# Hybrid attention and convolution layer: values loaded in shared chunks of three rows, and the order of the side work in the input projection

## The chip, the cores and the metric

One core of a Trainium2 chip runs the whole layer. The metric is the device time in microseconds (us) of one execution. The profile used here is of one execution of the same program.

## The reference

The layer takes 2048 latent tokens (a grid of 32 rows of 64) of width 1024 and 256 context tokens, all in float32:

```python
hx = modulate(rms_norm(x, norm1_g), sh1, sc1)
hc = modulate(rms_norm(ctx, norm1_g), csh1, csc1)
qx, kx, vx, ux = split_proj(hx @ w_in)              # 512, 512, 512 and 1024 columns
kc, vc = split_heads(hc @ w_in[:, 512:1536])
attn_x = neighbourhood_attention(rope(qx), qx, rope(kx), vx, kc, vc, rpb)
conv_x = conformer_conv(ux, dw_kernel, dw_bias, conv_ln_g, conv_ln_b)
x = x + g1 * (concat([attn_x, conv_x]) @ w_out)
x = x + g2 * (relu(modulate(rms_norm(x, norm2_g), sh2, sc2) @ w_mlp1) ** 2 @ w_mlp2)
out = rms_norm(x, final_g)
```

In the attention each token of row r attends to a window of 8 rows by 16 columns around it, with a learned bias by relative place (rpb), and to all 256 context keys, in one softmax. The convolution is a depthwise one of width 31 over the tokens, after a gated unit and before a LayerNorm. The vectors sh, sc and g come from products with w_ada.

## The kernel before

Float32 operands are split into a high and a low half, and each product is three matmuls (`mm3`, lines 90 to 92). The program has three stages: the input projection, the attention, and the output projection with the MLP. All data loads and stores stand in one queue, that of SyncE (SP), and are issued in its order.

**Input projection.** The tokens form two blocks of 1024 (b = 0, 1), each of two halves of 512 (`hf`). For each block the loop goes over ten groups of weight columns: four u groups (gated unit), two q, two k, two v; `half(gi, hf)` computes one group for one half. A half of a u group is 96 matmuls of 256 columns, a half of a q or k group 48 of 512 columns. Results go to DRAM: `h_d` (input of the convolution), `q_d`, `k_d`, `v_d`. Between the main matmuls stands side work:

- The convolution (`Conv`) works on pieces of 98 tokens by a Fourier transform: `load` reads a piece of h_d into `cw` and splits it on ACT and DVE (lines 416 to 418), `fwd` and `inv` are matmuls, `turn` transposes and stores. One piece is advanced in each half of q, k and v. `conv_tables` loads the transform's tables (`dftr`, `dwr`) and makes their product at line 396.
- `bias_tables` and `bias_rows` make tables of the attention's bias in DRAM: for each of 8 heads two loads (`tb`), an addition on GpSimd (POOL) and four stores, and then twelve larger copies from DRAM to DRAM into `bias_d` (line 299).
- `ada_chunk` computes a modulation vector on DVE from 16 loads of w_ada (`wr`). `pump` takes steps of it from a list, at a rate per half given by RATE.
- `load_x_half` loads four tiles of x for the next half or block and normalises them.

The scratch tiles of most of this (`gtile`, tag G) share one ring of four buffers. A scheduler decides the place of each instruction on its engine.

**Attention.** `groups_` lists 64 pairs p = (pr, hf, g): head pair pr (4 of them), column half hf, and row group g of four rows (8 of them). Its window is 11 rows of 40 columns (8 rows in the first and the last group). For a pair PE does scores (lines 986 and 988), transposes of the probabilities (lines 1024 and 1044) and the products with the values (lines 1062 and 1064), spread over three steps of a software pipeline (CYCLE). The values of a pair are loaded by one DMA, in chunks of three rows (120 partitions):

```python
v = ap.tile([P, 4, 2, P], F32R, tag="v", bufs=4, name=f"v{pr}{hf}{g}")
n = (nr + 2) // 3
src = v_d[hf * VW + r0 * 40:hf * VW + r0 * 40 + n * 120, pr * 256:(pr + 1) * 256]
```

r0 is 0 for the first group, 4g-4 for the others, so that the windows of neighbouring groups overlap by seven rows, and each loads its own copy. The queries of a pair (`q`, three buffers) are loaded two pairs ahead, the values one pair ahead (`loads`). The same queue also carries the next head pair's keys (`kr`), the bias tiles, and the stores of the results (`at_d`).

Of the kernel before, what the change touches and what calls it, by code (L numbers as in the profile page):

```python
# [18 lines left out]
P = 128  # L19
# [22 lines left out]
def hybrid_layer(ctx: ExitStack, tc: tile.TileContext, a: dict, out: bass.AP):  # L42
# [225 lines left out]
    def bias_tables():  # L268
# [4 lines left out]
        cm = gtile([64, 40], F32, "cm")  # L273
        SY.dma_start(cm, a["colmask"])
        neg = gtile([64, 120], F32, "neg")
        GE.memset(neg, NEG)
        SY.dma_start(z_d[0:32 * ZL].rearrange("(c l) -> c l", c=32)[:, 0:120 * 96],
                     rp_d.rearrange("a b -> (a b)").partition_broadcast(32))
        tiv = ti_d.rearrange("h f c n -> f c h n")
        for q in range(8):  # L280
            tb = gtile([64, 15, 40], F32, f"tb{q}")
            for hf in range(2):
                off = 32 + 15 - 8 * hf + q * 15 * 96
                src = z_d[off:off + 32 * (ZL - 1)].rearrange("(c l) -> c l", c=32)[:, 0:15 * 96]
                SY.dma_start(tb[hf * 32:hf * 32 + 32, :, :],
                             src.rearrange("c (h x) -> c h x", x=96)[:, :, 0:40])
            GE.tensor_tensor(tb, tb, cm.unsqueeze(1).broadcast_to([64, 15, 40]), ALU.add)
            for hf in range(2):
                src = tb[hf * 32:hf * 32 + 32, :, :].rearrange("p r c -> p (r c)")
                SY.dma_start(tf_d[q, hf], src)  # L290
                SY.dma_start(ti_d[q, hf][:, 120:440], src[:, 120:440])
# [93 lines left out]
    def conv_tables():  # L385
        ab = pa.tile([P, 2, 512], F32, name="cab")
# [6 lines left out]
        SY.dma_start(raw_[0:CW, 1, 0:2 * P], a["dft_k"])  # L393
        pt = psA("pab")
# [7 lines left out]
        z = gtile([P, 512], F32, "hz")  # L402
        GE.memset(z, 0.0)
        SY.dma_start(h_d[0:PAD], z[0:PAD])
        SY.dma_start(h_d[PAD + S:HR], z[0:HR - PAD - S])
        held = []
        cvc.update(ab=ab, br=br, hl=hl, held=held, ps=psA("pcv", held))

    class Conv:
# [47 lines left out]
    def conv_a(last):  # L457
        i = cv_pos[0]
        for d, fn in ((2, Conv.turn), (1, Conv.inv)):
            if cvc and 0 <= i - d < last and not hasattr(cvs[i - d], f"did{d}"):  # L460
                setattr(cvs[i - d], f"did{d}", True)
                fn(cvs[i - d])

    def conv_b(last):
# [7 lines left out]
        if i < last + 2:  # L472
            cv_pos[0] += 1
# [46 lines left out]
    def load_x_half(b, hf):  # L520
        tiles = []
        for i in range(4):
# [10 lines left out]
            tiles.append(xt)  # L533
        scale, shift = norm_mod(tiles, Ar, Br, f"n{b}{hf}")
# [142 lines left out]
    def before(gi):  # L677
# [3 lines left out]
        if gi == 0:  # L681
            xt1 = load_x_half(0, 1)
# [13 lines left out]
    def half(gi, hf):  # L696
# [3 lines left out]
        if kind == "u":  # L700
# [13 lines left out]
            if ct == 3 and hf == 1:  # L714
                cv_pos[0] = (0, CB0)[b]
                conv_b(CBS[b])
        elif kind in "qk":
            pt = psA(f"p{kind}{b}{idx}{hf}")
            for j in range(2):
                (conv_a, conv_b)[j](CBS[b])  # L720
# [3 lines left out]
            rope_store(b, kind, idx, hf, pt)  # L724
        else:
            for t2 in range(2):
# [4 lines left out]
                (conv_a, conv_b)[t2](CBS[b])  # L731
                if idx == 1 and hf == 1 and b + 1 < NB:
                    trans_half(pend["x"], b + 1, 0, (2 * t2, 2 * t2 + 1))
                v_tiles([getter(2 * t2), getter(2 * t2 + 1)], row, wget, idx, f"{b}{idx}{hf}{t2}")
        if gi == 1 and hf == 0:
            trans_half(xt1, 0, 1)
            in_order(n_start, (VE.engine, SE.engine, GE.engine))
        if kind == "v" and idx == 1 and b + 1 < NB and hf == 1:
            TH[1] = None
            pend["x"] = load_x_half(b + 1, 1)  # L740
# [14 lines left out]
        if gi == 3 and hf == 0:  # L755
            bias_tables()
        if gi == 2 and hf == 0:
# [12 lines left out]
    def after(gi):  # L770
# [101 lines left out]
    SC0 = 440  # L872
# [63 lines left out]
    def load_q(pr, hf, g):  # L936
        q = ap.tile([P, 2, 2, P], F32R, tag="q", bufs=3, name=f"q{pr}{hf}{g}")
# [3 lines left out]

    def load_v(pr, hf, g):
        r0, nr = geom(g)
        v = ap.tile([P, 4, 2, P], F32R, tag="v", bufs=4, name=f"v{pr}{hf}{g}")
        n = (nr + 2) // 3

        src = v_d[hf * VW + r0 * 40:hf * VW + r0 * 40 + n * 120, pr * 256:(pr + 1) * 256]
        SY.dma_start(f(v)[0:120, 0:n].rearrange("p c h d -> p c (h d)"),
                     src.rearrange("(c p) n -> p c n", p=120))
        VT[pr, hf, g] = v  # L950
# [3 lines left out]
    for bt_ in bias_t:  # L954
        GE.memset(bt_[:, SC0:696], 0.0)
# [13 lines left out]

    st_ = {}  # L970
# [6 lines left out]
    def qk(p, hd):  # L977
# [11 lines left out]
        st_[p, hd] = {"s": s, "c0": SC0 - nw, "nw": nw, "nch": (nr + 2) // 3, "nr": nr}  # L989

    def addmax(p, hd):
        pr, hf, g = groups_[p]
        d = st_[p, hd]
        c0, nw = d["c0"], d["nw"]
        bt = BT[pr, hf, typ(g), hd]
        sb = ap.tile([P, 696], F32, tag="S", bufs=7, name=f"sb{p}_{hd}")

        mn = ap.tile([P, 1], F32, tag="mn", bufs=4, name=f"mn{p}_{hd}")
        VE.tensor_tensor_reduce(sb[:, c0:696], d["s"][:, 512 - nw:768], bt[:, c0:696], -1.0, 3e38,  # L999
# [564 lines left out]
```

## Time and profile before

| | |
|---|---|
| median of three runs | 2643.2 us (2641.68 to 2648.05) |
| the profiled execution | 2637.4 us, span 2635.6 us |
| PE busy | 2450.8 us, 93% of the span |
| DVE, ACT, POOL busy | 1781.4, 1253.5, 1471.7 us |
| first scores of the attention | 682.9 us |
| mean granted clock of TensorE | 0.97 |

The first line of times is from runs without a profile. The span runs from the first to the last instruction. PE busy counts a matmul as busy however slowly it goes: a stretch with a low granted clock (PEclk) looks busy too, so that the clock is read beside it. Times in the rows below are us from the start of the span.

### The profile page before, as it was taken

The page shows a single profiled execution, that of the slowest core. Times are in us where ns is not written, and L with a number is a line of the kernel's source. Part 1 is how long each engine was busy: PE and PEld are TensorE (multiplying, and loading weights), DVE is VectorE, ACT ScalarE, POOL GpSimd, SP SyncE. Part 2 cuts the span into 40 slices and gives each one's busy share as a digit, 9 for nine tenths or more (in the row PEclk, how much of TensorE's full clock was granted, in tenths as well). Part 3 has the DMA queues.
Part 4 walks back from the last instruction along what each step waited for, and adds up shares of the span by engine and source line. Part 5 has one row for each costly group of instructions (what it writes and reads, how often), then busy time and mean ns, then how long its engine had stood idle before and what let it go on. Part 6 is the DMA issues. An engine that isn't in the chain of part 4 may idle for free.

```text
span 2635.6 us, 42228 instructions
## 1 busy us (share of the span) xinstructions
PE 2450.8 (93%) x15903; PEld 2228.9 (85%) x15903; DVE 1781.4 (68%) x2464; ACT 1253.5 (48%) x2166; POOL 1471.7 (56%) x1049
## 2 busy tenths in 40 slices
PE   7895999999788988998999989999999999899997
PEld 5883789879778888998899878999889999799996
DVE  6515853465578885648766688666797667877666
ACT  5324442354468773214544455444555444544442
POOL 3435614452467764537665566555675565765564
PEclk9997999999899999999999999999999999999999
DMA  8549572463899997566333344333353333433331
GB/s 307 168 121 294 171 224 83 119 177 109 203 239 250 255 225 196 177 208 224 124 101 97 108 137 131 101 103 101 104 161 103 104 105 112 136 112 104 99 94 56
DMA packets 303434, 398.38 MB, mean 151 GB/s; under 512 B 36694, under 2 KB 240781, under 8 KB 303197
## 3 DMA queue, kind: packets, MB, share of 16 engines
q1 hardware_dynamic: 303212, 395.68, 51.8%
q8 instruction: 125, 2.05, 0.3%
q14 instruction: 81, 0.66, 0.1%
q10 hardware_dynamic: 16, 0.00, 0.0%
HBM read 319.17 MB, written 86.76 MB: 154 GB/s over the span
## 4 chain that ended last, share of the span: by engine, by line
PE 64%; DMA 15%; DVE 9%; issue 4%; POOL 3%; SPq 1%; ACT 1%; DVEq 0%; POOLq 0%; ACTq 0%
PE pall L90 20%; PE pall L91 19%; PE pall L92 19%; DMA q<-q_d 7%; DMA wr<-in_w_ada 2%; PE pall L986 1%; DVE s L1353 1%; DVE ac L1456 1%; DVE ada L497 1%; PE pall L1024 1%; PE pall L1062 1%; DMA kr<-k_d 1%; DVE ac L1452 1%; DVE w L1378 1%; POOL w L1348 1%
## 5 line engine op out<-in xcount | busy, mean ns | idle before, releaser
L90 PE MATMUL pall<-w,hh 128*128 128x512 f32 x1024 | 407.1, 398 | 12.2 <-DVE ac L1452 7.2
L91 PE MATMUL pall<-w,hh 128*128 128x512 f32 x1024 | 404.4, 395 | 0.0
L92 PE MATMUL pall<-w,hl 128*128 128x512 f32 x1024 | 398.2, 393 | 0.6 <-DVE hl L1409 0.6
L1452 DVE TENSOR_TENSOR ac<-pall,ac 128x1024 f32<-128x1024 f32 x239 | 286.2, 1213 | 71.1 <-PE pall L92 71.0
L90 PEld LDWEIGHTS pall<-w,hh 128*128 128x128 f32 x1024 | 195.5, 191 | 53.0 <-issue 4.4
L92 PEld LDWEIGHTS pall<-w,hl 128*128 128x128 f32 x1024 | 194.4, 190 | 42.3 <-DVE hl L1409 2.1
L91 PEld LDWEIGHTS pall<-w,hh 128*128 128x128 f32 x1024 | 195.3, 191 | 36.7 <-issue 0.2
L86 POOL TENSOR_TENSOR w_0l<-w_0r,w_0h 128x1024 fp32r<-128x1024 f32 x20 | 51.7, 2586 | 193.2 <-ACT w_0h L85 193.2
L1406 ACT ACTIVATE c<-c 128x512 f32<-128x512 f32 x128 | 80.9, 632 | 162.6 <-DVE c L1426 134.9
L1017 POOL TENSOR_SCALAR sb<-sb,ri 128x696 f32<-128x696 f32 (+1 forms) x128 | 105.6, 826 | 89.2 <-DVE ri L1012 71.9
L90 PE MATMUL pall<-xah,w 128*128 128x256 f32 x512 | 145.0, 284 | 2.8 <-ACT w L1347 2.8
L92 PE MATMUL pall<-xah,w 128*128 128x256 f32 x512 | 145.4, 284 | 0.0
L91 PE MATMUL pall<-xal,w 128*128 128x256 f32 x512 | 145.1, 284 | 0.0
L999 DVE CUSTOM_DVE_ANT_0 sb<-pall,bias 128x696 f32<-128x696 f32 (+1 forms) x128 | 108.1, 845 | 44.6 <-PE pall L988 43.0
L1409 DVE TENSOR_TENSOR hl<-c,hh 128x512 fp32r<-128x512 f32 x128 | 123.6, 965 | 16.4 <-ACT hh L1408 16.2
L986 PE MATMUL pall<-kt,q 128*128 128x440 f32 (+1 forms) x256 | 75.1, 375 | 47.5 <-DMA q<-q_d 47.1
L1007 ACT ACTIVATE sb<-sb,mn 128x696 f32<-128x696 f32 (+1 forms) x128 | 109.7, 857 | 3.3 <-DVE mn L999 3.3
L1031 ACT CAST pw<-pall 120x512 fp32r<-120x512 f32 (+1 forms) x128 | 72.5, 568 | 76.2 <-PE pall L1024 66.6
L90 PEld LDWEIGHTS pall<-xah,w 128*128 128x128 f32 x512 | 98.4, 193 | 5.6 <-ACT w L1347 3.0
L91 PEld LDWEIGHTS pall<-xal,w 128*128 128x128 f32 x512 | 98.8, 193 | 2.9
L92 PEld LDWEIGHTS pall<-xah,w 128*128 128x128 f32 x512 | 98.8, 193 | 2.1
L1062 PE MATMUL pall<-pw,v 120*128 120x256 f32 (+1 forms) x480 | 92.7, 314 | 0.8 <-ACT ob L1069 0.8
(852 smaller groups left out, 8824.3 us busy)
## 6 DMA issues: line engine op xcount, KB each, us to landing
v<-v_d SPq DMA_DIRECT2D x48, 480.0 KB
q<-q_d SPq DMA_DIRECT2D x64, 256.0 KB
wr<-in_w_ada SPq DMA_DIRECT2D x48, 256.0 KB
v_d<-vt SPq DMA_DIRECT2D x64, 160.0 KB
wa<-in_w_ada SPq DMA_DIRECT2D x8, 1024.0 KB
x<-in_x SPq DMA_DIRECT2D x16, 512.0 KB
kr<-k_d SPq DMA_DIRECT2D x32, 256.0 KB
at_d<-ao SPq DMA_DIRECT2D x32, 256.0 KB
```

Source lines behind the costliest of these rows:

```text
L90: TE.matmul(outp, lh, rh, start=start, stop=False)
L91: TE.matmul(outp, lh, rl, start=False, stop=False)
L92: TE.matmul(outp, ll, rh, start=False, stop=stop)
L986: TE.matmul(s[:, 512 - nw:512], q[:, hd, 1, :], win, start=(z == 0), stop=(z == 1))
L999: VE.tensor_tensor_reduce(sb[:, c0:696], d["s"][:, 512 - nw:768], bt[:, c0:696], -1.0, 3e38, ALU.add, ALU.min, mn)
L1007: SE.activation(pb[:, c0:696], pb[:, c0:696], AF.Exp, bias=d["mn"], scale=-1.0, accum_out=d["sm"])
L1017: GE.tensor_scalar(pb[:, c0:696], pb[:, c0:696], d["ri"], 1.0, ALU.mult, ALU.mult)
L1031: SE.copy(d["pw"][0:120, 0:nch, 0, :], d["tv"])
L1062: TE.matmul(o, v[0:n, ch, hd, :], pw[0:n, ch, :, :], start=(ch == 0), stop=False)
L1406: SE.activation(c, c, AF.Relu)
L1409: VE.tensor_tensor(dl, cv, f(dh), ALU.subtract)
L1452: VE.tensor_tensor(ac, po_, ac, ALU.add)
```

## The change

In the attention, `chunks(hf, g)` gives the chunks of three rows that hold a group's window. Where r0 leaves remainder 0 or 1 by three, chunks are cut at multiples of three rows and kept in `VT` under their row, so that a later group uses those that are loaded already; with remainder 1 the window begins one row into its first chunk, and the probabilities of that row are zeros in the score tile, which now has 40 columns more. Groups with remainder 2 (g = 3 and 6) load four chunks of their own. Each chunk has a DMA and a tile of its own. Values are loaded two pairs ahead and queries three.

In the input projection the loads of the convolution's tables are issued earlier and their product made later; a piece's split is moved from `load` to just before `fwd`; the bias tables are made one head per half during q and k, and `bias_rows` follows in v (BR0 from 6 to 9); loading x and normalising it are separate steps; the three modulation vectors begin at groups 9, 10 and 12 in place of 3, 5 and 7, at a lower rate.

```diff
-    def bias_tables():
+    def bias_start():
...
+    def bias_head(q):
+        tb = gtile([64, 15, 40], F32, f"tb{q}")
...
+    def bias_end():
...
+    def conv_loads():
...
+        z = gtile([P, 512], F32, "hz")
+        VE.memset(z, 0.0)
...
         def load(self):
             self.w = pa.tile([P, 2, 512], F32R, tag="H", bufs=3, name=f"cw{self.i}")
             SY.dma_start(f(self.w)[:, 0, :], h_d[self.t0:self.t0 + P])
+
+        def split(self):
             SE.copy(self.w[:, 1, :], f(self.w)[:, 0, :])
...
+    def conv_at(d, last):
+        i = cv_pos[0] - d
+        if 0 <= i < last and not hasattr(cvs[i], f"did{d}"):
+            setattr(cvs[i], f"did{d}", True)
+            (Conv.inv, Conv.turn)[d - 1](cvs[i])
+
+    def conv_end(last):
         i = cv_pos[0]
         if i < last:
-            if i == 0 or i == CB0:
-                cvs[i].load()
+            cvs[i].split()
             cvs[i].fwd()
             if i + 1 < last:
                 cvs[i + 1].load()
...
-    BR0 = 6
+    BR0 = 9
     adas = {ch: ada_chunk(ch) for ch in (2, 3, 4)}
-    RATE = {"u": (9, 6), "q": (6.5, 4), "k": (6.5, 4), "v": (7.5, 6)}
+    G0 = NG // NB
+    ADA = {G0 - 1: 2, G0: 3, G0 + 2: 4}
+    RATE = {"u": (5.2, 6), "q": (5.2, 4), "k": (5.2, 4), "v": (5.2, 6)}
...
         if gi == 3 and hf == 0:
-            bias_tables()
-        if gi == 2 and hf == 0:
+            bias_start()
+            bias_end()
+        if 4 <= gi < 8:
+            bias_head((gi - 4) * 2 + hf)
+        if gi == 1 and hf == 1:
+            conv_loads()
+        if gi == 2 and hf == 1:
             conv_tables()
...
-        q = ap.tile([P, 2, 2, P], F32R, tag="q", bufs=3, name=f"q{pr}{hf}{g}")
+        q = ap.tile([P, 2, 2, P], F32R, tag="q", bufs=4, name=f"q{pr}{hf}{g}")
...
+    def chunks(hf, g):
+
+        r0, nr = geom(g)
+        o = r0 % 3
+        if o == 2:
+            return [((hf, g, i), r0 + 3 * i, 40 * min(3, nr - 3 * i)) for i in range(4)], 0
+        n = -(-(nr + o) // 3)
+        return [((hf, r0 // 3 + i), r0 - o + 3 * i, 40 * min(3, nr + o - 3 * i)) for i in range(n)], o
+
     def load_v(pr, hf, g):
...
+        for key, r, n in chunks(hf, g)[0]:
+            key = (pr, *key)
+            if key in VT:
+                continue
+            own = len(key) == 4
+            n = 40 * min(3, ROWS - r)
+            VT[key] = v = ap.tile([P, 2, P], F32R, tag="vo" if own else "v", bufs=8 if own else 12,
+                                  name="v" + "_".join(map(str, key)))
+            SY.dma_start(f(v)[0:n].rearrange("p h d -> p (h d)"),
+                         v_d[hf * VW + r * 40:hf * VW + r * 40 + n, pr * 256:(pr + 1) * 256])
...
+        if 0 < p < NP - 3:
+            load_q(*groups_[p + 3])
         if 0 < p < NP - 2:
-            load_q(*groups_[p + 2])
-        if 0 < p < NP - 1:
-            load_v(*groups_[p + 1])
+            load_v(*groups_[p + 2])
```

The scheduler's order shows three places. The first is PE's order in the third u group of block 0 (w_0 and w_1 are the weights' two parts, t00 and t01 the two halves of tokens, h and l the high and low halves). Before:

```order
L396 MATMUL pall<-dwr,dftr 128x512 x2
L91 MATMUL pall<-w_1l,t01h 128x256
L92 MATMUL pall<-w_1h,t01l 128x256
L90 MATMUL pall<-w_1h,t01h 128x256
L91 MATMUL pall<-w_1l,t01h 128x256
```

And of the changed kernel:

```order
L409 MATMUL pall<-dwr,dftr 128x512 x2
L90 MATMUL pall<-w_0h,t00h 128x256
L91 MATMUL pall<-w_0l,t00h 128x256
L92 MATMUL pall<-w_0h,t00l 128x256
L90 MATMUL pall<-w_0h,t00h 128x256
```

The tables' product has moved from the middle of the second half of this group (after 43 of its 96 matmuls) to its end. The second place is SP's queue in the first halves of q in block 0, where `cw` is a piece of the convolution's input. Before, from the third piece:

```order
L416 DMA cw_1514<-h_d 128x512
L299 DMA bias_d_81<-tf_d 16x32x320
L299 DMA bias_d_82<-ti_d 16x32x440
L451 DMA cv_d<-ccx_1609 128x4x98
L598 DMA q_d<-qh0q_1546 64x2x512
L598 DMA q_d<-ql0q_1547 64x2x512
L598 DMA q_d<-qh0q_1546 64x2x512
L598 DMA q_d<-ql0q_1547 64x2x512
L299 DMA bias_d_83<-tf_d 16x32x320
L83 DMA w_1r<-in_w_in 128x4x256
L299 DMA bias_d_81<-tf_d 16x32x320
```

And of the changed kernel, from the same piece:

```order
L425 DMA cw_1508<-h_d 128x512
L610 DMA q_d<-qh0q_1467 64x2x512 x2
L610 DMA q_d<-ql0q_1468 64x2x512 x2
L610 DMA q_d<-qh0q_1483 64x2x512 x2
L285 DMA tb_1510<-z_d 32x15x40
L610 DMA q_d<-ql0q_1484 64x2x512 x2
L285 DMA tb_1510<-z_d 32x15x40
L462 DMA cv_d<-ccx_1518 128x4x98
L83 DMA w_0r<-in_w_in 128x4x256
L290 DMA tf_d<-tb_1510 32x600
L291 DMA ti_d<-tb_1510 32x320
L290 DMA tf_d<-tb_1510 32x600
```

The copies into bias_d have left this stretch (they now stand among the stores of v, twelve within sixteen rows of the order), and one head's tb loads and tf_d and ti_d stores have come into each half. The third place is SP's queue at the fourth to sixth pair of the attention, where 64x1024 loads are keys. Before:

```order
L939 DMA q_5878<-q_d 128x4x128
L948 DMA v_5880<-v_d 120x4x256
L939 DMA q_5924<-q_d 128x4x128
L948 DMA v_5926<-v_d 120x4x256
L623 DMA v_d<-vt_5737 40x2x512 x4
```

And of the changed kernel, with a pair that brings one new chunk and one that brings four of its own:

```order
L966 DMA q_6017<-q_d 128x4x128
L990 DMA v_1_4_6019<-v_d 120x256
L836 DMA kr_6021<-k_d 64x1024 x2
L966 DMA q_6084<-q_d 128x4x128
L990 DMA v_0_3_0_6086<-v_d 120x256
L990 DMA v_0_3_1_6088<-v_d 120x256
L990 DMA v_0_3_2_6090<-v_d 120x256
L990 DMA v_0_3_3_6092<-v_d 120x256
```

One load of four chunks per pair has become none to four loads of one chunk. CYCLE, which orders a pair's work on PE, DVE, ACT and POOL, is unchanged.

## Rows read from the trace of the kernel before

**Rows 1.** The page: its first line, and the chain that ended last, by line.

```profile
span 2635.6 us, 42228 instructions
...
PE pall L90 20%; PE pall L91 19%; PE pall L92 19%; DMA q<-q_d 7%; DMA wr<-in_w_ada 2%; PE pall L986 1%; DVE s L1353 1%; DVE ac L1456 1%; DVE ada L497 1%; PE pall L1024 1%; PE pall L1062 1%; DMA kr<-k_d 1%; DVE ac L1452 1%; DVE w L1378 1%; POOL w L1348 1%
```

**Rows 2.** Waits of PE: total us, times, longest.

```profile
PE pall L986 <- DMA q<-q_d: 47.1, 31, 4.5
PE pall L90 <- ACT cw L417: 21.5, 2, 17.4
...
PE pall L396 <- DMA dftr<-in_dft_k: 9.9, 1, 9.9
```

**Rows 3.** Windows: length, busy PE, PEld, DVE, ACT, POOL, PEclk, DMA share, GB/s.

```profile
107.20:119.60 12.40, 11.70 (x98) 11.50 (x96) 9.21 (x7) 3.53 (x4) 11.24 (x4) 1.00 0.66 215
119.60:147.70 28.10, 18.16 (x101) 15.44 (x102) 3.73 (x5) 1.51 (x2) 0.75 (x2) 0.70 0.41 137
170.70:325.20 154.50, 118.90 (x484) 89.28 (x482) 100.96 (x124) 66.19 (x113) 91.32 (x49) 0.87 0.76 220
233.30:270.80 37.50, 12.61 (x27) 7.64 (x28) 24.80 (x27) 13.27 (x27) 19.24 (x12) 0.50 0.82 254
491.00:575.80 84.80, 81.68 (x376) 65.70 (x375) 60.12 (x81) 44.69 (x86) 49.29 (x31) 1.00 0.62 180
325.20:393.50 68.30, 62.37 (x462) 58.52 (x461) 41.05 (x60) 32.39 (x57) 11.23 (x4) 0.95 0.71 222
```

**Rows 4.** SP's timeline, 214 to 252 us: start, length, line, DMA.

```profile
225.14 5.76 SPq L299 DMA_DIRECT2D bias_d<-tf_d  x2
...
250.17 0.55 SPq L416 DMA_DIRECT2D cw<-h_d  x1
```

**Rows 5.** DMA issues from 203 to 236 us.

```profile
bias_d<-tf_d SPq DMA_DIRECT2D x8, 640.0 KB
bias_d<-ti_d SPq DMA_DIRECT2D x4, 880.0 KB
```

**Rows 6.** The bias tables' tile tb: ns least/median/most, first and last start.

```profile
L290 SPq DMA_DIRECT2D tf_d<-tb x16: 313/412/483, 177.2 to 200.6; - x16
...
L287 POOL TENSOR_TENSOR tb<-tb,cm x8: 1459/1476/1492, 175.7 to 197.0; 64x600 f32<-64x600 f32 x8
```

**Rows 7.** Windows of the attention, columns as in rows 3.

```profile
683.00:771.00 88.00, 68.68 (x466) 64.64 (x466) 59.98 (x154) 56.19 (x123) 49.83 (x76) 0.90 1.06 233
771.00:845.40 74.40, 66.10 (x496) 63.31 (x496) 62.33 (x158) 59.03 (x129) 53.34 (x80) 0.98 1.07 248
845.40:921.40 76.00, 66.19 (x496) 63.40 (x496) 62.31 (x158) 58.58 (x128) 51.63 (x78) 0.98 1.06 251
921.40:1004.00 82.60, 71.91 (x527) 69.35 (x528) 65.79 (x162) 62.11 (x134) 54.00 (x82) 0.94 0.93 222
971.50:991.40 19.90, 19.90 (x162) 19.69 (x161) 19.26 (x49) 18.47 (x41) 16.80 (x26) 1.00 0.99 230
```

**Rows 8.** PE's timeline: first scores of pairs 0, 10, 11 and 63.

```profile
682.90 0.53 PE L986 MATMUL pall<-kt,q 128*128 128x320 f32 x2 [3.41 <-DMA q<-q_d]
...
743.51 0.67 PE L986 MATMUL pall<-kt,q 128*128 128x440 f32 x2 [0.59 <-DMA q<-q_d]
...
747.64 0.56 PE L986 MATMUL pall<-kt,q 128*128 128x440 f32 x2
...
991.44 0.46 PE L986 MATMUL pall<-kt,q 128*128 128x320 f32 x2
```

**Rows 9.** DMA issues of the whole run: loads of the values.

```profile
v<-v_d SPq DMA_DIRECT2D x48, 480.0 KB
...
v<-v_d SPq DMA_DIRECT2D x16, 360.0 KB
```

**Rows 10.** SP's issues in the attention (tiles v and bias): ns least/median/most.

```profile
L948 SPq DMA_DIRECT2D v<-v_d x62: 323/542/3610, 689.7 to 987.6; - x62
...
L967 SPq DMA_DIRECT2D bias<-bias_d x42: 319/384/2364, 683.6 to 935.0; - x42
```

More of the change, by code (lines that the diff above doesn't have):

```diff
@@ L272, in bias_tables @@
         SY.dma_start(rp_d, rp)
-        cm = gtile([64, 40], F32, "cm")
-        SY.dma_start(cm, a["colmask"])
+        bt_["cm"] = pa.tile([64, 40], F32, name="cm")
+        SY.dma_start(bt_["cm"], a["colmask"])
+        SY.dma_start(z_d[0:32 * ZL].rearrange("(c l) -> c l", c=32)[:, 0:120 * 96],
+                     rp_d.rearrange("a b -> (a b)").partition_broadcast(32))
+    def bias_head(q):
+        tb = gtile([64, 15, 40], F32, f"tb{q}")
+        for hf in range(2):
+            off = 32 + 15 - 8 * hf + q * 15 * 96
+            src = z_d[off:off + 32 * (ZL - 1)].rearrange("(c l) -> c l", c=32)[:, 0:15 * 96]
+            SY.dma_start(tb[hf * 32:hf * 32 + 32, :, :],
+                         src.rearrange("c (h x) -> c h x", x=96)[:, :, 0:40])
+        GE.tensor_tensor(tb, tb, bt_["cm"].unsqueeze(1).broadcast_to([64, 15, 40]), ALU.add)
+        for hf in range(2):
+            src = tb[hf * 32:hf * 32 + 32, :, :].rearrange("p r c -> p (r c)")
+            SY.dma_start(tf_d[q, hf], src)
+            SY.dma_start(ti_d[q, hf][:, 120:440], src[:, 120:440])
+    def bias_end():
         neg = gtile([64, 120], F32, "neg")
         GE.memset(neg, NEG)
-        SY.dma_start(z_d[0:32 * ZL].rearrange("(c l) -> c l", c=32)[:, 0:120 * 96],
-                     rp_d.rearrange("a b -> (a b)").partition_broadcast(32))
         tiv = ti_d.rearrange("h f c n -> f c h n")
[L280 to L291, printed above, removed]
         for hf in range(2):
@@ L454, in hybrid_layer @@
     cv_pos = [0]
[L457 to L464, printed above, removed]
+    def conv_at(d, last):
[4 more added lines that the diff above has]
+    def conv_end(last):
         i = cv_pos[0]
         if i < last:
-            if i == 0 or i == CB0:
-                cvs[i].load()
+            cvs[i].split()
             cvs[i].fwd()
@@ L471, in conv_b @@
                 cvs[i + 1].load()
-        if i < last + 2:
-            cv_pos[0] += 1
+        cv_pos[0] += 1
     def ada_chunk(ch):
@@ L715, in half @@
                 cv_pos[0] = (0, CB0)[b]
-                conv_b(CBS[b])
+                cvs[cv_pos[0]].load()
+                conv_end(CBS[b])
         elif kind in "qk":
@@ L739, in half @@
             TH[1] = None
-            pend["x"] = load_x_half(b + 1, 1)
+            pend["x"] = x_half(b + 1, 1)
+        if b > 0 and kind == "u" and idx == 0 and hf == 0:
+            norm_half(pend["x"], b, 1)
+        if b + 1 < NB and kind == "q" and idx == 1 and hf == 0:
+            norm_half(pend["x"], b + 1, 0)
         if b > 0 and kind == "u" and idx == 1 and hf == 0:
@@ L968, in load_b @@
         BT[key] = bt
+    score_t = deque(ap.tile([P, SE_], F32, name=f"sb{i}") for i in range(7))
+    for sb_ in score_t:
+        GE.memset(sb_[:, 0:40], 0.0)
     st_ = {}
@@ L1006, in expo @@
         d["sm"] = ap.tile([P, 1], F32, tag="sm", bufs=4, name=f"sm{p}_{hd}")
-        SE.activation(pb[:, c0:696], pb[:, c0:696], AF.Exp, bias=d["mn"], scale=-1.0, accum_out=d["sm"])
+        SE.activation(pb[:, c0:SE_], pb[:, c0:SE_], AF.Exp, bias=d["mn"], scale=-1.0, accum_out=d["sm"])
     def recip(p, hd):
@@ L1016, in norm @@
         c0, pb = d["c0"], d["pb"]
-        GE.tensor_scalar(pb[:, c0:696], pb[:, c0:696], d["ri"], 1.0, ALU.mult, ALU.mult)
+        GE.tensor_scalar(pb[:, c0:SE_], pb[:, c0:SE_], d["ri"], 1.0, ALU.mult, ALU.mult)
     def tr_win(p, hd):
         d = st_[p, hd]
-        c0, nch, pb = d["c0"], d["nch"], d["pb"]
+        c0, pb = d["c0"] - 40 * d["ch"][1], d["pb"]
         t = TW[:, hd * 512:(hd + 1) * 512]
-        for ch in range(nch):
+        for ch in range(len(d["ch"][0])):
             TE.transpose(t[0:120, ch * P:(ch + 1) * P], pb[:, c0 + 120 * ch:c0 + 120 * ch + 120], ident)
@@ L1138, in hybrid_layer @@
             load_b(*groups_[p], hd)
-    load_v(*groups_[0])
+    for p in range(2):
+        load_v(*groups_[p])
     n_att = len(nc.cur_bb.bb.instructions)
-    load_q(*groups_[2])
-    load_v(*groups_[1])
     for p in (2, 3):
+        load_q(*groups_[p])
+        if p == 2:
+            load_v(*groups_[p])
         for hd in range(2):
```

66 lines of the change are left out of this document (32 added, 34 removed).

## The prediction

> **What bounds the kernel now.** Read the page first: the span, and what ended last. The chain is mostly matmuls, but one load stands in it with 7% of the span, the queries from DRAM [rows 1]. So PE is the engine to follow, and the next view is what PE waited for: 47.1 us for queries, 21.5 us for two pieces of the convolution (one of them 17.4 us), 9.9 us for the convolution's tables [rows 2]. These three stand in the two stages that the diff touches. The rest of the run, from 1004 us on, keeps its code and order, and I count it as unchanged.
>
> Then read windows, stage by stage, with the granted clock beside the busy time. In the projection an ordinary half of a u group takes 12.4 us [rows 3]. The half with the tables' product takes 28.1 us at a clock of 0.70: PE waits, and then runs at the lower of its two levels (1.2 in place of 2.4 GHz) for some time. The eight halves of q and k of block 0 take 154.5 us, 19.3 us each; the first six of block 1, with the same matmuls and one convolution piece each, take 84.8 us, 14.1 us each, at full clock [rows 3]. The worst of block 0 lies between 233 and 271 us: 37.5 us at half clock with PE busy for 12.6. SP's timeline tells why. The piece that PE waits for is issued at 250.17 us, behind a queue in which two copies into bias_d alone held SP for 5.76 us [rows 4]. Twelve such copies, 8640 KB, were issued from 203 to 236 us [rows 5].
>
> In the attention the four head pairs' windows show the DMA engines at a share of 1.06 to 1.07 in the first three, and 0.93 in the last [rows 7]: they are full. A pair that finds its queries there takes 4.13 us (743.51 to 747.64), and the mean over 63 pairs is (991.44 - 682.90) / 63 = 4.90 us [rows 8]. No other engine sets the slower pace: between 971.5 and 991.4 us five pairs pass at 3.98 us each with PE busy all the time, though DVE is busy for 19.26 and ACT for 18.47 of those 19.90 us [rows 7].
>
> **The tables' product.** Its loads are issued earlier, and the product stands 53 matmuls later. The half of 28.1 us should become one of 12.4 plus the product itself, four matmuls; I take 2 us for these. Gain 28.1 - 12.4 - 2 = 13.7 us.
>
> **Block 0's q and k.** Without the burst of copies and without the ada steps, these halves resemble block 1's: 8 x 14.13 = 113.1 us in place of 154.5, a gain of 41.4 us. Two things come in and are not in block 1's window. First, a head of the bias tables per half: six DMAs, of which the tf_d stores hold SP for 0.41 us each [rows 6], so 2.5 us of SP, and one addition of 1.48 us on POOL. POOL was busy for 49.3 of 84.8 us in block 1's window, 8.2 us per half; with the addition it is 9.7 of 14.1, still beside PE's matmuls. On SP the stores wait for the addition, and behind them in the queue stand the next q stores and the convolution's next piece, for which PE waits in turn. If that cover is gone a half costs 2.5 us more, 20 us in all; if it holds, nothing. The neighbours in the queue are needed a half later, so I take 1 us per half, 8 us. Second, the burst is not gone but moved into v of block 0, four halves in 68.3 us [rows 3]. It fills the DMA engines for about the 33 us that it took before. What may be late there are the stores of v, and with them the scratch ring: four buffers at one buffer per 8.5 us (68.3 / 8) last 34 us, about as long as the burst. If that cover fails, PE stalls as it did at 233 us: 37.5 us, less the 12.6 busy ones at half speed, is 31 us lost. If it holds, nothing; I take 6 us. The moved ada steps fall on block 1's u groups; a u half that carried such steps had DVE busy for 9.21 of 12.4 us with PE at 11.70 [rows 3], so I cost them at nothing. The late split of a piece costs nothing while its load, a half ahead, has landed.
>
> Projection: 13.7 + 41.4 - 8 - 6 = 41 us. Bounds: 13.7 + 41.4 - 20 - 31 = 4 and 55 us.
>
> **The attention's loads.** Before, 48 loads of 480 KB and 16 of 360 KB [rows 9] are 28,800 KB. After, per head pair and column half, eleven shared chunks (the last of two rows, 80 KB) and eight own ones, 120 KB each: 2240 KB, times eight 17,920 KB, in 152 loads. The cut is 10,880 KB, 11.1 MB, 2.79 MB per head pair. Taken from each window at its own rate [rows 7], the DMA time becomes:
>
> - first: 88.0 us x 233 GB/s = 20.5 MB; 17.7 MB at the same rate take 76.0 us;
> - second: 18.45 - 2.79 = 15.7 MB at 248 GB/s, 63.2 us;
> - third: 19.08 - 2.79 = 16.3 MB at 251 GB/s, 64.9 us;
> - last: 18.3 - 2.79 = 15.5 MB at about 250 GB/s, 62 us.
>
> PE's own time, at 4.1 us per pair, is 65.6 us for sixteen; in the last window it is 15 x 4.1 plus the 12.6 us from 991.44 to 1004, 74.1 us. The larger of the two: 76.0 + 65.6 + 65.6 + 74.1 = 281 us, against 321. That is 40 us less. DMA and PE come out within 3 us of each other in the middle windows, so waits will not vanish; the queries' extra pair of lead covers most, and I keep back 5 us: 35 us. Bounds: if fewer bytes help only half as much, 20; if every pair runs at 4.1 us, 308.5 - 258.3 = 50 us.
>
> What it adds: 88 more DMAs on SP. A bias load, of nearly the same size, holds SP for a median of 0.38 us, a value load for 0.54 [rows 10]; by the larger, 88 x 0.54 = 48 us over 64 pairs, 0.74 us in each 4.1. It lies beside PE's work, since queries are now three pairs ahead; with that cover gone it would be those 48 us. At each change of head pair two chunks wait for a buffer that is read two pairs earlier, in the step in which SP asks for it; behind them stand later queries and keys, and one step (4.1 us) is less than the lead. The zeroed 40 columns are seven short memsets.
>
> The Trainium skill speaks against this part: "DMA: Bandwidth & Descriptors", section "Anatomy of one DMA", gives each transfer about 2.0 us fixed plus bytes at 436 GB/s, by which, as an estimate, a 480 KB load takes 3.1 us and four of 120 KB 9.1. Paid one after the other that is a loss and not a gain; what that would do here is rival 4, worked out from rows. The trace does not bear it out so far: bias loads of 160 KB hold the queue for 0.38 us at the median [rows 10], with the DMA engines full.
>
> **Sum.** 41 + 35 = 76 us from the profiled execution's 2637.4 us gives 2561. The median of the timed runs is 5.8 us above that execution; on its scale the forecast is 2643.2 - 76 = 2567 us.
>
> **The rivals.**
>
> 1. *The burst stalls v instead.* For it: 8640 KB at the same rate in a stretch with DMA already at a share of 0.71 [rows 3]. Against: no convolution piece is queued behind most of it. The projection then gains 41 - 25 = 16 us: 2643 - 51 = 2592 us.
> 2. *The attention stays as it is*, because small loads keep the DMA engines as long as large ones. For it: a share of 1.07 tells that they are full, not what fills them. Against: the three full windows carry different other loads, and all move 233 to 251 GB/s [rows 7]. 2643 - 41 = 2602 us.
> 3. *All waits go*: 55 + 50 = 105 us, 2538 us.
> 4. *Slower: SP becomes the attention's bound.* A value load now and then held SP for up to 3.61 us [rows 10]. With 2.4 loads per pair and some 1.45 us for the three other DMAs at about 0.5 us, a pair reaches 6.4 us if each small load holds SP for 2.1 us, halfway between the median and the longest. That is 1.5 x 63 = 95 us more, 2643 + 95 - 41 = 2697 us. It decides against the change from 1.7 us per load on: (4.90 + 41/63 - 1.45) / 2.4. The median is 0.54.
>
> **How the numbers follow.** About 0.3% (8 us) is what a measurement of this kernel tells from no change. Forecast 0.62; rival 1 0.13; rival 2 0.10; rival 3 0.09; rival 4 0.04; gains and losses that cancel 0.02. Faster: 0.94; within 0.3%: 0.02; slower: 0.04. The likeliest case alone spans 2550 to 2590. The range goes from rival 3 to just beyond rival 2: 2538 to 2608 us.
>
> **What would show it.** The tables' product without a wait; block 0's q and k in about 121 us; first scores near 642 us; PE's wait for queries in the attention below 15 us with the DMA share under 1; 64 pairs in about 275 us. The prediction is wrong if v of block 0 grows beyond 80 us, if a wait for v or for SP's issue takes the queries' place, or if the DMA share stays at 1.07 with fewer bytes.

## The result, and the profile after

The changed kernel takes 2572.5 us (median of four runs, 2562.6 to 2575.3) against 2642.4 us for the kernel before on the same chip: a ratio of 0.973, 95% interval 0.9703 to 0.9757. The forecast was 2567 us. The profiled execution takes 2570.7 us. Its page begins so, and its chain by line answers to [rows 1]:

```profile
span 2568.9 us, 42313 instructions
...
PE pall L90 18%; PE pall L91 18%; PE pall L92 18%; PE pall L1105 2%; PE pall L1069 1%; PE pall L1030 1%; DVE s L1398 1%; DMA ar<-at_d 1%; DVE ac L1501 1%; DVE ac L1497 1%; PE pall L1107 1%; DVE w L1423 1%; PE pall L1032 1%; DMA cw<-h_d 1%; DMA xn_d<-xo 1%
```

The queries' load is gone from the chain. PE's waits in the changed kernel (total us, times, longest) answer to [rows 2]:

```profile
PE pall L91 <- DVE cyl L439: 10.4, 4, 6.5
...
PE pall L227 <- POOL x L221: 6.6, 4, 2.8
PE pall L1069 <- POOL sb L1062: 6.6, 5, 3.9
...
PE pall L90 <- DVE br L518: 5.3, 1, 5.3
...
PE pall L1030 <- DMA q<-q_d: 2.3, 3, 0.9
...
PE pall L90 <- ACT cw L428: 1.8, 1, 1.8
```

Queries fell from 47.1 to 2.3 us, the convolution's piece from 21.5 to 1.8, and the wait for the tables is gone. In their place stand waits for VectorE and GpSimd, all smaller but for one kind: `cyl`, `x` and `br` belong to side work that the diff moved.

PE's timeline gives the first scores of the first and the last pair, which answer to the outer two of [rows 8]:

```profile
665.95 0.53 PE L1030 MATMUL pall<-kt,q 128*128 128x320 f32 x2 [0.67 <-DMA q<-q_d]
...
927.63 0.46 PE L1030 MATMUL pall<-kt,q 128*128 128x320 f32 x2
```

So the span's 66.7 us (2635.6 to 2568.9) split into 17.0 before the first scores (682.90 to 665.95), 46.9 between the two (308.5 to 261.7), and 2.9 behind them (1644.2 to 1641.3). The forecast had 41 and 35, and nothing for the rest.

Windows of the attention by head pair, with the columns of [rows 3], answer to [rows 7]:

```profile
665.95:733.51 67.56, 61.71 (x466) 59.44 (x466) 59.94 (x155) 56.64 (x122) 47.98 (x70) 0.97 0.99 255
733.51:804.16 70.65, 64.73 (x496) 63.03 (x497) 61.28 (x156) 58.61 (x127) 53.63 (x81) 0.98 1.05 254
804.16:867.71 63.55, 62.16 (x498) 61.36 (x497) 61.23 (x160) 58.54 (x129) 53.00 (x79) 1.00 0.92 252
867.71:927.63 59.92, 58.59 (x468) 57.76 (x467) 57.79 (x148) 55.07 (x121) 49.78 (x74) 1.00 0.68 190
```

Two things can be seen. The last two head pairs run at PE's own pace (59.9 us for 15 pairs is 3.99 us each). And in the first window the share is down from 1.06 to 0.99 while the rate is *up*, from 233 to 255 GB/s: less share, more bytes per second. The forecast had kept the rate. The share did not fall below 1 everywhere, as it was to: the second window is still at 1.05, and takes 70.65 us, where 16 pairs at 4.0 take 64.

Windows of the projection (the half before the tables' product, the half with it, q and k of block 0, v of block 0, u of block 1, the first two q halves of block 1):

```profile
109.60:121.20 11.60, 11.60 (x99) 11.60 (x98) 11.18 (x6) 2.93 (x3) 11.50 (x4) 1.00 0.50 159
121.20:134.70 13.50, 13.50 (x102) 12.12 (x101) 3.72 (x6) 3.65 (x5) 2.52 (x2) 1.00 0.92 306
158.50:288.10 129.60, 110.93 (x473) 88.19 (x472) 89.77 (x102) 61.25 (x109) 87.00 (x47) 0.91 0.57 158
288.10:348.80 60.70, 57.16 (x458) 55.23 (x457) 33.56 (x47) 28.57 (x48) 12.16 (x7) 1.00 0.90 290
348.80:459.60 110.80, 104.50 (x813) 100.18 (x812) 40.26 (x40) 27.57 (x38) 32.32 (x13) 0.95 0.46 138
459.60:499.70 40.10, 29.67 (x124) 21.13 (x122) 30.09 (x38) 13.57 (x25) 21.77 (x12) 0.96 0.64 195
```

Block 1 in the kernel before, its u groups and its first two q halves:

```profile
393.50:491.00 97.50, 96.79 (x804) 96.27 (x804) 25.25 (x20) 22.05 (x28) 33.22 (x13) 1.00 0.26 78
491.00:518.20 27.20, 27.20 (x126) 22.11 (x125) 19.50 (x24) 14.38 (x25) 14.25 (x9) 1.00 0.44 122
```

Against these and [rows 3], the two halves around the tables' product give 15.4 us (12.4 and 28.1 to 11.6 and 13.5), q and k of block 0 give 24.9 (154.5 to 129.6), and v 7.6 (68.3 to 60.7), although v now carries the copies (share 0.90). Then block 1 gives back: its u groups take 110.8 us where they took 97.5, its first two q halves 40.1 where they took 27.2. The rest is 4.7 us later in sum. 15.4 + 24.9 + 7.6 - 13.3 - 12.9 - 4.7 = 17.0.

### The profile page after: what moved, and what is told of

Same layout as the page of the kernel before. It is cut to its first block, busy times and chain, and to the rows that moved or that the text cites. A ratio compares the mean times of both kernels' runs of the same rounds, so it can differ in the third digit from the quotient of the medians.

```text
span 2568.9 us, 42313 instructions
## 1 busy us (share of the span) xinstructions
PE 2430.5 (95%) x15903; PEld 2216.9 (86%) x15903; DVE 1790.2 (70%) x2465; ACT 1248.7 (49%) x2162; POOL 1467.8 (57%) x1055
## 4 chain that ended last, share of the span: by engine, by line
PE 62%; DVE 10%; DMA 9%; POOL 5%; issue 4%; SPq 2%; ACT 1%; DVEq 0%; POOLq 0%; ACTq 0%
PE pall L90 18%; PE pall L91 18%; PE pall L92 18%; PE pall L1105 2%; PE pall L1069 1%; PE pall L1030 1%; DVE s L1398 1%; DMA ar<-at_d 1%; DVE ac L1501 1%; DVE ac L1497 1%; PE pall L1107 1%; DVE w L1423 1%; PE pall L1032 1%; DMA cw<-h_d 1%; DMA xn_d<-xo 1%
## 5 line engine op out<-in xcount | busy, mean ns | idle before, releaser
L1451 ACT ACTIVATE c<-c 128x512 f32<-128x512 f32 x128 | 80.9, 632 | 157.2 <-DVE c L1471 129.2
L90 PE MATMUL pall<-xth,w 128*128 128x256 f32 x256 | 75.2, 294 | 19.1 <-DVE pu L1459 19.1
L1081 DVE TENSOR_TENSOR pw<-pall,pw 120x512 fp32r<-120x512 f32 (+1 forms) x128 | 83.5, 653 | 5.1 <-ACT pw L1076 4.7
```

The source lines that it names most:

```text
L90: TE.matmul(outp, lh, rh, start=start, stop=False)
L1081: VE.tensor_tensor(pw[0:120, 0:nch, 1, :], d["tv"], f(pw)[0:120, 0:nch, 0, :], ALU.subtract)
L1451: SE.activation(c, c, AF.Relu)
```

## The experiments

Each run has its own before on the same chip, 2638 to 2642 us in the median.

**1. The attention's part alone** (the projection as before):

> The kernel before with the attention's part of the change alone (shared chunks, values two and queries three pairs ahead). Theory: the two parts add up, and by the two profiles the attention's is 308.5 - 261.7 = 47 us from the first to the last scores, so about 2596 us, with PE's wait for queries under 5 us. Rival: part of that gain needs the projection's part (an emptier queue at the start of the attention), and this kernel gains under 30 us (2612 or more).

2588.8 us, ratio 0.9802 (0.9774 to 0.9829). First to last scores 263.9 us, and PE waits 3.7 us for queries. The rival, a gain under 30 us, falls; the gain is 7 us more than the theory's.

**2. The projection's part alone** (the attention as before):

> The kernel before with the input projection's part alone. Theory: it brings the first scores from 683 to about 666 us, a gain of 17 to 20 us, about 2624 us, with block 0's q and k near 130 us and block 1's u and first q 26 us longer than before. Rival: the gain is 41 us as forecast, and the rest is lost only together with the new attention: 2602 us.

2623.0 us, ratio 0.9932 (0.9905 to 0.9959), with block 0's q and k at 129.2 us and block 1's u at 111.4. The parts add up: 0.9802 x 0.9932 = 0.9735. By the medians they are worth 52 and 17 us; in the profiled executions the attention is 45 us shorter in run 1 (308.5 to 263.9) and the first scores 15 us earlier in run 2 (682.9 to 667.7). The attention gave more than forecast, the projection less than half.

**3. Shared chunks without the longer lead.** Queries are asked for two pairs ahead, values one:

```diff
-        if 0 < p < NP - 3:
-            load_q(*groups_[p + 3])
         if 0 < p < NP - 2:
-            load_v(*groups_[p + 2])
+            load_q(*groups_[p + 2])
+        if 0 < p < NP - 1:
+            load_v(*groups_[p + 1])
```

> The kernel before with shared chunks, but values one pair and queries two pairs ahead as before. Theory: the DMA engines were full, and 11.1 MB less is what frees the pairs: at least 30 us of the 47, about 2605 us, with the wait for queries under 15 us. Rival: the lead does it: under 15 us gained (2628 or more), with the queries still waited for 30 us or more.

2592.3 us, ratio 0.9818 (0.9791 to 0.9846); PE waits 15.5 us for queries, just above the theory's 15. Nearly all of the attention's gain is in this part.

**4. The longer lead without shared chunks** (the same lines the other way, in the kernel before):

> The kernel before with the longer lead alone (four query buffers, five value buffers of four chunks), each pair still loading its own values: no byte less. Theory (bytes): DMA share stays at 1.06 and at most 10 us are gained, 2633 us or more. Rival (lead): 30 us or more gained, 2613 us or less.

2647.0 us, ratio 1.002 (1.0003 to 1.0037): no gain, as the theory had it; the DMA share from 700 to 900 us is 1.05. The view of all engines' waits from the first to the last scores shows where the queries' wait went:

```profile
POOL ao L1078 <- DMA at_d<-ao: 58.2, 19, 8.5
...
PE pall L1024 <- POOL sb L1017: 34.9, 20, 4.6
PE pall L986 <- DMA q<-q_d: 14.8, 8, 4.1
```

The first of these in the kernel before, where PE waited for `sb` for 0.2 us in all:

```profile
POOL ao L1078 <- DMA at_d<-ao: 17.5, 10, 4.0
```

The earlier loads stand in the queue ahead of the store of the attention's output; GpSimd waits for that store before it may write the next `ao`, its `sb` is late behind it, and PE waits for `sb`. With the DMA engines this full, the longer lead only chose which transfer was late.

**5. The longer lead, with each pair's values chunk by chunk.** The same bytes as in run 4, 240 loads in place of 64:

```diff
-        SY.dma_start(f(v)[0:120, 0:n].rearrange("p c h d -> p c (h d)"),
-                     src.rearrange("(c p) n -> p c n", p=120))
+        for c in range(n):
+            SY.dma_start(f(v)[0:120, c].rearrange("p h d -> p (h d)"), src[c * 120:(c + 1) * 120])
```

> The kernel before with queries and values asked for one pair earlier (as in the run with the longer lead alone) and each pair's values loaded chunk by chunk, in 240 loads of 120 KB in place of 64 large ones, with the same bytes. It measures what small loads cost by themselves. Theory (the bytes count, and SP has room for the issues): 176 more issues at 0.38 to 0.54 us are 67 to 95 us of SP beside 315 us of attention, and the time stays within 10 us of the run with the longer lead alone, 2637 to 2657. Rival (each small load holds the queue or the DMA engines for about 2.1 us): 3.75 loads per pair, 7.9 us, and 1.45 us for the other loads give 9.3 us per pair in place of 4.9, so 2850 or above; at half that price, 1.05 us, the pairs are at 5.4 us and the time near 2680.

2615.2 us, ratio 0.9902 (0.9878 to 0.9925). Neither theory had this: 32 us *faster* than run 4 with no byte less. Bytes were not all that the shared chunks had changed, so my account of run 3 was open again.

**6. Chunk by chunk at the lead of before** (the edit of run 5, in the kernel before):

> The kernel before, in which each pair's values are loaded chunk by chunk, in 240 loads of 120 KB in place of 64 large ones; the same bytes, the lead of before. The run with small loads and the longer lead was 32 us faster than the one with the longer lead alone, which fewer bytes cannot explain. Theory 1 (fewer bytes make the attention faster, and small loads help only where the lead is longer): first to last scores stay at 300 to 308 us, the time within 8 us of 2641. Theory 2 (the form of the loads counts: chunk by chunk, the same bytes pass faster): first to last scores take 270 to 285 us, the time is 2605 to 2618, and of the 48 us that sharing brought at the old lead the cut in bytes is worth the smaller part, some 15 to 25 us.

2611.6 us, ratio 0.989 (0.986 to 0.9919); first to last scores 284.2 us (681.49 to 965.73). Theory 2 holds.

**7. As many small loads, but in strips.** Each load has 30 partitions by four chunks (or 40 by three):

```diff
-        SY.dma_start(f(v)[0:120, 0:n].rearrange("p c h d -> p c (h d)"),
-                     src.rearrange("(c p) n -> p c n", p=120))
+        m = 120 // n
+        for s in range(0, 120, m):
+            SY.dma_start(f(v)[s:s + m, 0:n].rearrange("p c h d -> p c (h d)"),
+                         src.rearrange("(c p) n -> p c n", p=120)[s:s + m])
```

> The kernel before, in which each pair's values are loaded in strips of 30 partitions by four chunks (40 by three), so in as many loads of 120 KB as chunk by chunk, with the same bytes; but each load still takes its rows from four places in DRAM, as the large load does, in the same order on a partition. It separates the size of a load from the order of its addresses. If the size of one load counts: within 8 us of the run chunk by chunk. If the order counts (rows of one chunk stand together in DRAM, and so their packets are shorter): the packets of 1 KB are as long as in the kernel before (72 ns and more) and the time is within 8 us of 2641, or above it for the 176 further issues.

2654.2 us, ratio 1.0052 (1.0034 to 1.0071). Small loads by themselves are not enough. The DMA queue's view of the same 200 us (700 to 900) in four kernels (packets, MB, packets' time as a share of 16 engines) shows what differs. Before:

```profile
q1 hardware_dynamic: 54006, 48.43, 105.9%
```

Strips, run 7:

```profile
q1 hardware_dynamic: 48307, 42.92, 98.4%
```

Chunk by chunk, run 6:

```profile
q1 hardware_dynamic: 60905, 52.10, 100.3%
```

Shared chunks, run 3:

```profile
q1 hardware_dynamic: 57887, 49.20, 95.4%
```

The mean time of a packet is share x 16 x 200 us / packets: 62.7 ns before, 65.2 in strips, 52.7 chunk by chunk and 52.7 with shared chunks. That is 16% less chunk by chunk. A part is the mix: the mean packet has 897 bytes before and 855 chunk by chunk, and for the same bytes the packets take 12% less time. It is not the value loads' alone: in the packets of these traces, those of 512 bytes, nearly all of them the queries', whose load is the same in runs 6 and 7 as before, take 40.3 ns before, 42.2 in strips and 34.1 chunk by chunk; those of 1 KB, most of them values, 68.2, 72.2 and 58.7. With loads of one chunk other loads' packets pass faster too; sharing then lowers the number of packets. So of the 48.2 us of run 3 (2640.5 - 2592.3), about 30 are the form of the loads (run 6, 2641.8 - 2611.6 = 30.2; 21 to 37 by its interval) and the other 18, by difference, the fewer bytes and loads. What in the form it is, the runs don't separate: a large load and a strip go from chunk to chunk, 120 rows of `v_d` apart, on each partition in turn, and a chunk load takes neighbouring rows across 120 partitions; a strip is also narrower than both, so that a gain by small size could be hidden by the width.

**8. The copies into bias_d later, in the kernel before.** They are issued in block 1's u groups:

```diff
-    BR0 = 6
+    BR0 = 10
...
-            bias_rows(gi - BR0)
+            sp = [i for i in nc.cur_bb.bb.instructions[-400:] if i.engine == SY.engine]
+            with tc.issue_after(sp[-1]):
+                bias_rows(gi - BR0)
```

> The kernel before, in which only the twelve copies into bias_d (8640 KB) are issued later, in block 1's u groups in place of block 0's q and k. Theory (the burst makes block 0's q and k slow): the eight halves of q and k of block 0 fall from 154.5 us to 120 to 130, as in the changed kernel (129.6), and block 1's u groups pay for it what they cost in the changed kernel at most, from 97.5 to some 110 us; first scores some 15 us earlier, about 668, and the time about 2627. Rival (the ada steps and the chain of GpSimd and VectorE behind each piece make these halves slow, and the burst lies beside them): they stay above 145 us, the first scores at 683 or later, the time 2642 or above.

2623.4 us, ratio 0.9929 (0.9913 to 0.9945). Windows (block 0's q and k; block 1's u; its first two q halves):

```profile
169.00:309.50 140.50, 115.82 (x485) 87.74 (x483) 102.43 (x124) 65.71 (x113) 93.44 (x49) 0.91 0.65 179
...
378.40:475.30 96.90, 96.19 (x802) 95.77 (x802) 24.55 (x19) 21.03 (x26) 32.49 (x13) 1.00 0.55 169
475.30:502.50 27.20, 27.20 (x129) 22.15 (x127) 14.15 (x22) 11.43 (x20) 15.64 (x9) 1.00 0.50 148
```

The copies cost block 0's q and k 14 us, no more (the theory had 25 to 35, the rival at most 10), and block 1's u nothing. This one edit gives what the whole projection part gives (17 us). The stage's other 27 us over block 1's pace were not the copies'.

**9. The copies later in the changed kernel** (the edit of run 8):

> The changed kernel, in which only the twelve copies into bias_d are issued later, in block 1's u groups in place of block 0's v. Theory (the burst delays the stores of v and with them the scratch ring, GpSimd's shifts of x and the transposes, 11 us at 360 to 383 us): the wait in that place goes, the next u halves take some of it back; first scores 5 to 11 us earlier, the time 2562 to 2568. Rival (the moved ada steps and the moved norm of the second x half make block 1's u slow, whatever the DMA engines carry): block 1's u stays at 110 us and the time within 4 us of 2572; if the burst is worse there than in v, above 2576.

2573.1 us, ratio 0.9731 (0.9711 to 0.9751). Windows (v of block 0; u of block 1):

```profile
288.80:346.40 57.60, 56.94 (x457) 55.18 (x456) 31.79 (x47) 32.44 (x54) 12.16 (x7) 1.00 0.65 203
346.40:458.90 112.50, 104.21 (x811) 99.01 (x810) 35.50 (x37) 23.83 (x31) 31.13 (x12) 0.95 0.60 186
```

v gains the 3 us that the copies cost it; u stays slow. The rival holds: what block 1 loses is not the copies' doing.

**10. The ada steps back where they were:**

```diff
-    ADA = {G0 - 1: 2, G0: 3, G0 + 2: 4}
-    RATE = {"u": (5.2, 6), "q": (5.2, 4), "k": (5.2, 4), "v": (5.2, 6)}
+    ADA = {3: 2, 5: 3, 7: 4}
+    RATE = {"u": (9, 6), "q": (6.5, 4), "k": (6.5, 4), "v": (7.5, 6)}
```

> The changed kernel with the ada steps at the places and rates of before (in block 0's u, q and k, in place of block 1's u). Theory (the moved ada steps cost 10 to 13 us in block 1's first q halves, where PE waits for the third chunk's last product): these two halves fall from 40.1 to about 28 us; block 0's q and k, which get the steps back, rise from 129.6 by 0 to 8 us; the first scores come 5 to 13 us earlier, the time 2560 to 2567. Rival (the steps cost as much in block 0 as in block 1): block 0's q and k rise by 10 us or more and the time stays at 2570 to 2580.

2578.5 us, ratio 0.9761 (0.9743 to 0.9779). Windows (q and k of block 0; u of block 1; its first two q halves):

```profile
155.80:296.20 140.40, 116.91 (x481) 88.59 (x479) 109.83 (x116) 61.69 (x108) 92.04 (x48) 0.93 0.61 169
...
360.00:486.80 126.80, 104.58 (x809) 100.16 (x808) 34.81 (x32) 28.96 (x39) 32.37 (x13) 0.89 0.37 115
486.80:514.00 27.20, 27.20 (x126) 22.08 (x125) 18.63 (x25) 13.44 (x24) 15.18 (x10) 1.00 0.46 137
```

The q halves fall to 27.2, as the theory says: their 12.9 us are the ada steps'. But q and k of block 0 rise by 10.8 us, which is the rival, and u by 16, where PE now waits for the steps' products. Its waits from 360 to 490 us:

```profile
PE pall L514 <- DVE ada L506: 19.8, 2, 11.2
```

**11. Copies later, ada steps and the second half's norm as before:**

```diff
-            pend["x"] = x_half(b + 1, 1)
-        if b > 0 and kind == "u" and idx == 0 and hf == 0:
-            norm_half(pend["x"], b, 1)
+            pend["x"] = norm_half(x_half(b + 1, 1), b + 1, 1)
```

> The changed kernel with three things of its projection put back or elsewhere: the twelve copies into bias_d in block 1's u groups (as in the run of before with late copies, which gained 17 us), the ada steps and their rates as before, and the norm of block 1's second x half straight after its load as before. Theory (block 1's u and first q halves lose 26 us by the moved norm and ada steps, and the copies cost nothing in block 1's u where these are not beside them): block 1's u takes 97 to 100 us and its first two q halves 27 to 29; block 0's q and k 135 to 141; first scores 645 to 652; time 2553 to 2560. Rival (the stretch at 360 to 383 us comes from the later split of the pieces, the shorter tables' half or from the order of x's loads, not from norm or ada): block 1's u stays at 108 us or more and the time above 2564.

2569.9 us, ratio 0.9726 (0.9702 to 0.9751), not to be told from the changed kernel. Windows (q and k; v; u; first two q halves):

```profile
156.70:296.90 140.20, 117.09 (x481) 89.03 (x479) 109.61 (x116) 61.67 (x108) 92.28 (x48) 0.91 0.61 169
296.90:372.10 75.20, 63.20 (x462) 58.31 (x461) 48.15 (x67) 33.09 (x58) 11.72 (x5) 0.95 0.75 221
372.10:469.00 96.90, 96.19 (x802) 95.77 (x802) 23.01 (x19) 21.74 (x28) 32.48 (x13) 1.00 0.55 169
469.00:496.10 27.10, 27.10 (x127) 22.08 (x126) 13.94 (x22) 11.44 (x20) 15.62 (x9) 1.00 0.50 149
```

For block 1 the theory is right: it is back at 96.9 and 27.1. The time is not, because I left out v: with the norm and the steps back, it takes 14.5 us more than in the changed kernel, and q and k 10.6 more. Here the side work that left one stage was paid in another.

**12. The ada steps in block 0's v**, the rest as in run 11:

```diff
-    ADA = {3: 2, 5: 3, 7: 4}
+    ADA = {7: 2, 8: 3, 9: 4}
```

> The kernel of the run before this one (late copies, old norm, old rates), with the ada steps moved once more: into block 0's v groups and the group behind them, in place of block 0's q and k. From block 0's q on, to the second q half of block 1, that run took 339.4 us and the changed kernel 341.2 us. Theory (block 0's q and k pay 11 us for the steps, v without the copies has room for them): q and k 128 to 133 us, v 75 to 80, block 1's u and first q halves 124 to 126, so 327 to 339 in all and a time of 2557 to 2570, faster than the changed kernel by up to 15 us. Rival (wherever the 48 ada steps stand in the projection, they cost some 11 to 13 us, since VectorE and GpSimd already hold up the convolution's pieces there): v rises by as much as q and k fall, the four stages take 338 us or more and the time is 2566 to 2580.

2562.0 us (2559.9 to 2566.7), ratio 0.9709 (0.9681 to 0.9738): the fastest median. Each against its own before, it is 0.2% (some 5 us) below the changed kernel, and the intervals overlap: not to be told from it. Windows (q and k; v; u with the first two q halves):

```profile
156.10:285.10 129.00, 111.36 (x472) 88.35 (x471) 89.82 (x102) 61.25 (x109) 87.59 (x47) 0.92 0.57 158
285.10:344.70 59.60, 58.89 (x462) 55.43 (x460) 31.78 (x47) 35.02 (x60) 12.04 (x6) 1.00 0.64 202
...
344.70:487.90 143.20, 128.36 (x926) 119.22 (x925) 75.29 (x70) 30.64 (x42) 49.73 (x21) 0.95 0.62 191
```

The four stages end at 487.9 us and take 331.8, as the theory has it in sum. Their division is another: no cost came up in v, and u with the first q halves takes 143.2 us in place of 125 (124.0 in run 11). So the steps slow block 1's u even with the norm at its old place, here beside the copies. One wait in PE's timeline there:

```profile
381.47 2.79 PE L227 MATMUL pall<-ident,x 128*128 128x128 f32 x12 [11.74 <-DVE sg L725]
```

VectorE's `sg` stood behind an ada step that had waited 8.3 us for its load.

## Why the prediction was right, and where it was not

That the time fell within 6 us of the forecast is luck. In the profiled executions the span fell by 66.7 us, not 76: the projection gave 17 us in place of 41, the attention 46.9 in place of 35, and 2.9 came from behind it, where none was expected. Two errors of opposite sign, with nothing in common, made the sum look better than its terms.

**The tables' product** was right: 15.4 us against 13.7. The wait is gone and the product costs 1.9 us (13.5 less 11.6).

**Block 0's q and k** was mis-sized: 24.9 us in place of 41.4 - 8 = 33. The step that failed is "without the burst and without the ada steps, these halves resemble block 1's". Runs 8 and 10 give the parts, 14 us for the copies and 11 for the steps, together the 24.9. The price of 8 us for the eight heads is not measured by any run: in the kernel before all eight additions stood in this stretch too, at its start (175.7 to 197.0 us, [rows 6]), and so they do in run 8:

```profile
L287 POOL TENSOR_TENSOR tb<-tb,cm x8: 1461/1477/1490, 174.0 to 195.8; 64x600 f32<-64x600 f32 x8
```

Spreading them over the halves cost nothing beyond that (140.5 us in run 8, 140.4 in run 10, both with the steps); what they cost in either place stays open. No run shows what keeps these halves 16 us above block 1's pace, and the heads may be a part of it. The worst place in the changed kernel, in the timeline of all engines:

```profile
229.16 6.42 POOL L287 TENSOR_TENSOR tb<-tb,cm 64x600 f32<-64x600 f32 x1
...
229.41 4.86 DVE L218 SCALAR_TENSOR_TENSOR x<-x,n10ss,Ar 128x1024 f32<-128x1024 f32 x4
...
240.18 9.27 POOL L221 TENSOR_TENSOR x<-x,Br 128x1024 f32<-128x1024 f32 x4
...
242.54 9.34 DVE L439 TENSOR_TENSOR cyl<-cy,cyh 128x1024 fp32r<-128x1024 f32 x1 [5.82 <-ACT cyh L438]
...
251.94 0.74 PE L91 MATMUL pall<-cyl,chl 128*98 128x512 f32 x1 [6.50 <-DVE cyl L439]
```

A head's addition, 1.48 us in [rows 6], takes 6.42 while VectorE scales x; then `cyl` takes 9.34 us while GpSimd shifts x, and PE waits for it. I had counted POOL's busy time per half, and neither its order nor VectorE's work on the same data.

**The burst in v** (6 us) cost 3.1 by run 9; the cover that I doubted held, and rival 1 fell. In all v became 7.6 us shorter, for which the sum had no term. **The moved ada steps at nothing** is a wrong step, and the moved norm has no term at all. The steps cost block 1's q halves 12.9 us (run 10). The 13.3 of u are not the copies' (run 9), do not go with the steps alone (run 10), and go when copies, steps and norm are all moved (run 11). In the changed kernel's trace PE's transposes wait there for GpSimd's shifts of the moved norm (`x`, 6.6 us above), between 372 and 381 us, and no ada step runs on VectorE from 345 to 399 us; the granted clock of u is 0.95 in the mean, where it was 1.00. So the norm is the likelier cause there, but no run moves it alone, and run 12 loses as much with the norm in its old place. The cover that I named was VectorE's spare busy time in a u half of block 0. By the waits for `br` and `sg` it is not VectorE's share that is short: what PE waits for is late in its queue, or behind a load.

**The attention** was under-sized: 46.9 us against 35, near the bound of 50. The term that failed is the DMA time of each window, taken "at the same rate". The rate did not stay: packets took 16% less time, 12% for the same bytes. I had priced fewer bytes only, and some 30 of the part's 52 us are the form of the loads (run 6). The mechanism named, full DMA engines, was right; its measure was not: the rates at these shares, 233 to 251 GB/s, were no bound in bytes. Rival 2 (small loads keep the engines as long) fell, and the lead that was to cover the rest is worth nothing by itself (run 4) and 3.5 us on top of the shared chunks (2592.3 to 2588.8), within both intervals.

**Rival 4**, SP as the bound, fell. SP's issues of chunk loads in the changed kernel (least, median, most ns):

```profile
L990 SPq DMA_DIRECT2D v<-v_d x152: 309/361/1415, 663.7 to 915.3; - x152
```

0.36 us is below the 0.54 of a large load [rows 10], and far from the 1.7 from which it would decide. The Trainium skill's "DMA: Bandwidth & Descriptors" ("Anatomy of one DMA") has, for transfers that GpSimd issues, some 2.0 us fixed each. Paid one after the other it is not borne out here, where SP issues them: 240 loads in place of 64 were faster (run 6).

## What to carry to other kernels

Where the DMA engines are full, look at a packet's mean time before counting bytes: a load that takes neighbouring rows across all partitions may pass at a better rate than one that jumps (52.7 against 62.7 ns here), and may speed up the other loads beside it. Ask for transfers earlier only where there is room for them, and look which store then waits. When side work moves, price it by the queue it lands in (what stands behind it, and what the neighbouring engine does on the same data), not by the engine's free share.

## What was not expected of the hardware

Here VectorE and GpSimd kept each other waiting for whole instructions. `tb` took 6.42 us, about its own 1.48 and the 4.86 of VectorE's four scalings. `cyl` against its other instances (ns least, median, most, by its tile):

```profile
L439 DVE TENSOR_TENSOR cyl<-cy,cyh x21: 1206/1226/9344, 161.0 to 645.5; 128x1024 fp32r<-128x1024 f32 x21
```

The Trainium skill's "SBUF — State Buffer", section "Who interferes with whom", says that a VectorE instruction with two inputs in SBUF and a GpSimd instruction that reads SBUF share a read port, which the first holds for its whole instruction. The trace agrees as far as one instruction holds up the other. It shows more: `cyl`, begun 2.4 us after the first of the four shifts, ended only 2.4 us behind the last (251.88 against 249.45). GpSimd's next work is four subtractions (`ql0q`), of which the third, from 250.77 us, took 1.70 us in place of 0.72. By these times VectorE did not get in between the shifts, and came in only after two of the subtractions.

The second is the packet time of 62.7 against 52.7 ns when the same values are loaded in another form, and that the queries' packets, loaded as before, are shorter with it (40.3 to 34.1 ns). The cause stays open, as said under run 7.
